# A decoder trunk in split float32: a narrower second product behind the sub-layer borders, a shift split once a sub-layer, and another order of the output's chunks

## The chip, the cores and the metric

The kernel runs on one core of a Trainium2 chip. The time is the device time of one launch in microseconds (us), the median of several runs.

## The reference

Two layers over one sequence of 256 tokens of width 1024. Each layer has three sub-layers: a half-step SwiGLU FFN, a token mixer (layer 0: stick-breaking attention, layer 1: an RG-LRU recurrence) and a second FFN. Each sub-layer is normed and modulated by a conditioning vector `c`:

```python
def sublayer_input(x, g, mod_j):
    shift, scale, gate = mod_j[:, 0], mod_j[:, 1], mod_j[:, 2]
    h = rmsnorm(x, g) * (1 + scale[:, None, :]) + shift[:, None, :]
    return h, (1 + gate)[:, None, :]
...
    for layer in range(DEPTH):
        mod = (c_act @ mod_w[layer] + mod_b[layer]).reshape(B, N_SUB, 3, D_MODEL)
        h, g = sublayer_input(x, norm_g[layer, 0], mod[:, 0])
        x = x + MACARON_W * g * swiglu(h, ffn_w_gu[layer, 0], ffn_w_down[layer, 0])
        h, g = sublayer_input(x, norm_g[layer, 1], mod[:, 1])
        ...
        x = x + g * y
        h, g = sublayer_input(x, norm_g[layer, 2], mod[:, 2])
        x = x + MACARON_W * g * swiglu(h, ffn_w_gu[layer, 1], ffn_w_down[layer, 1])
    return rmsnorm(x, final_norm_g)
```

Everything is float32. About 250 MB of weights are read once.

## The kernel before

**Split products.** Activations lie with the features on the 128 partitions and the 256 tokens along the free axis. A float32 product is made of three products of a 32-bit format that TensorE streams faster ("fp32r"): each operand is split into a high part and a low part, and `group` (L610) issues high weights x high activations, high weights x low activations, low weights x high activations, all into one PSUM bank. Weights come by DMA into `raw`, ScalarE writes the high part `wh` (L581) and VectorE the low part `wl` (L584). Activations of a sub-layer's input are `hx` tiles (with copies of the first of them in `hk`), and what goes into a down projection lies in an arena, `arenar`: the FFN's products `y`, the attention's output, the recurrence's output.

**Borders.** Behind a sub-layer the norm's factor is not known until all of `x` is. `up_first` therefore multiplies the first two weight tiles of the next sub-layer with `x * scale` without the norm, and `evict` multiplies the result with the factor `rst` afterwards (`tr`, L857). The shift, which the norm's factor doesn't touch, rides along in two more columns: `scaled` writes 256 columns of `x * scale` and 2 columns of the shift, so these products have 258 columns (`TX`). ScalarE writes the two high columns, VectorE the two low ones (L720), once for each of the eight chunks of a sub-layer. `evict` reads one of the two result columns as the bias `bc` (L856). There are five such borders, (0,1), (0,2), (1,0), (1,1) and (1,2) as (layer, sub-layer). Each has 2 weight tiles x 8 chunks x 2 halves = 32 groups, 96 matmuls of 258 columns. Meanwhile `rstd` sums the squares, and `norm_chunk` makes the normed input for the weight tiles that follow: `hpre` (L730), its high part on ScalarE, its low part on VectorE (L737).

**The end.** `final` multiplies the eight chunks of `x` by the last norm's factor in five VectorE instructions (`put`, L1386) and stores each by DMA, in turn from SP's and ScalarE's queue.

**Order.** All operations are recorded, and `schedule` sets their order: a list scheduler with a cost for each operation (`c_act`, `c_dve`, `c_mm`) and due times. On ScalarE and VectorE it may hold an engine idle for a more urgent operation that is about to be ready (`wait_for`). TensorE's own order is as recorded.

**Where the tiles lie.** Tiles of the pool `const` are placed one behind the other in each partition, in the order of the listing, and the arena of each phase behind the last of them. Three tiles that nothing uses stand between them:

```python
HXPAD, HKPAD, ARPAD = 112, 16, 56
...
    const.tile([P, HXPAD], F32, tag="pad0", name="pad0")
    hxr, _ = ring("hx", 20, TX, F32R, pitch=320)
    const.tile([P, HKPAD], F32, tag="pad2", name="pad2")
    hkr, _ = ring("hk", 2, T, F32R)
...
    gbias = Buf(ap=fixed("gbias", KD))
    fixed("pad1", ARPAD)
```

In the built program a partition's bytes are: `wh` and `wl` from 43136 (a pitch of 4224, and a view that starts 0 or 128 bytes into the tile, so every one of their views starts at a multiple of 128), `hx` at 102720, `hk` at 128384, `ntri` at 164544, `none` at 165056, `gbias` at 167744, `arenar` at 168000.

Of the kernel before, what the change touches and what calls it, by code (L numbers as in the profile page):

```python
# [130 lines left out]
class Program:  # L131
# [58 lines left out]
    def schedule(self):  # L190
# [61 lines left out]
        def wait_for(e, t, o):  # L252

            q = queue[e]
            while head[e] < len(q) and q[head[e]].start is not None:
                head[e] += 1
            n, i = 0, head[e]
            slack = o.prio + late - t
            while n < LOOK and i < len(q):
                u = q[i]  # L260
                i += 1
                if u.start is not None:
                    continue
                n += 1
                if u is o or u.prio >= o.prio:
                    break
                g = guess(u, 3)
                if g is None or g >= t + o.cost or g <= t:
                    continue
                if u.prio + late - g < o.cost and u.prio + late - g < slack - MARGIN:  # L270
                    return g
            return None
# [123 lines left out]
def c_dve(n):  # L396
    return 68.0 + 1.042 * n
# [11 lines left out]
def trunk(ctx, tc, first_in, cb, par, modw, gu, wdn, qk, wv, wo, win, wri, wout, out):  # L409
# [12 lines left out]
    def f32(ap):  # L422
        return ap.bitcast(F32)
# [74 lines left out]
    def fixed(name, cols, dt=F32):  # L498
        return const.tile([P, cols], dt, tag=name, name=name)
# [51 lines left out]
    def A(o, i, f, n, r, w, table=None, psum=False, ptr=0, after=(), **kw):  # L551
        def fn():
            act.activation(o(), i(), f, **{k: (v() if callable(v) else v) for k, v in kw.items()})  # L553
        return pr.op("ACT", c_act(n, psum, ptr), fn, r, w, after, table)

    def V(fn, n, r, w, cost=None, ptr=0):
        return pr.op("DVE", cost or c_dve(n) + 62.0 * ptr, fn, r, w)

    def load(src, n, name, chain=None, sizes=None, plain=0, homes=(), behind=(), kind=Buf):

# [30 lines left out]
    class Acc:  # L591
# [3 lines left out]
            self.b = Buf(banks, name=name)  # L595
            self.started = False

        def group(self, part, o, w, wc, xs, xc, stop, parts=(None,), passes=(0, 1, 2)):

            b = self.b  # L600
            start = not self.started
            self.started = True
            wh, wl = w
            xh, xl = xs

            def fn():
                seq = ((wh, xh), (wh, xl), (wl, xh))
                for n, i in enumerate(passes):
                    u, v = seq[i]
                    pe.matmul(o(b()), wc(u()), xc(v()), start=start and n == 0, stop=stop and n == len(passes) - 1,  # L610
                              skip_group_check=True)

            n = xs_n[0]
            ws = [wh] * (passes != (2,)) + [wl] * (2 in passes)
            rd = ws + [(t, q) for t in [xh] * (passes != (1,)) + [xl] * (1 in passes) for q in parts]
# [15 lines left out]
    def group(acc, part, o, w, wc, xs, xc, n, stop, parts=(None,), passes=(0, 1, 2)):  # L631
        xs_n[0] = n
        return acc.group(part, o, w, wc, xs, xc, stop, parts, passes)


    def mod_tile(l, s, w, t, after=(), lat=None, rate=RATE, home=None, behind=()):
# [11 lines left out]
    def mod_final(l, s, w, t0=0, n=KD):  # L648
        m, f = mraw[l, s, w], mfin[l, s, w]
        b = OFF_MB + (l * 9 + s * 3 + w) * KD + t0  # L650
        rr = [(m, t) for t in range(t0, t0 + n)]
        ww = [(f, t) for t in range(t0, t0 + n)]
        pp = [(pars, 0)] if l == s == 0 else [pars]
        mi = lambda: m()[:, t0 : t0 + n]
        fo = lambda: f()[:, t0 : t0 + n]
        if w == 0:
            V(lambda: dve.tensor_tensor(fo(), mi(), col(b, n), ALU.add), n, rr + pp, ww)
# [10 lines left out]
    ssq, hcur, gcur, hkick = {}, {}, {}, {}  # L668

    def add_square(gen, d):  # L670
        if d == 0:
# [39 lines left out]

    def scaled(gen, d):

        gs, sh = mfin[gen + (1,)], mfin[gen + (0,)]
# [5 lines left out]
        V(lambda: dve.tensor_tensor(lo()[:, T:], shc(), f32(hi()[:, T:]), ALU.subtract), 2, [(sh, d), (hi, 1)], [(lo, 1)])  # L720
        A(lambda: hi()[:, :T], x[d], AF.Copy, T, [x[d], (gs, d)], [(hi, 0)], ptr=1, scale=lambda: gs()[:, c])
        V(lambda: dve.scalar_tensor_tensor(lo()[:, :T], x[d](), gs()[:, c], f32(hi()[:, :T]), ALU.mult, ALU.subtract), T,
          [x[d], (gs, d), (hi, 0)], [(lo, 0)], ptr=1)

    def norm_chunk(gen, d, q, whole=False):
        gs, sh = mfin[gen + (1,)], mfin[gen + (0,)]
        hp, hi, lo = Buf(hpr), Buf(hxr), Buf(hxr)
        hcur.setdefault(gen, []).append((hi, lo))
        c = slice(d, d + 1)
        V(lambda: dve.scalar_tensor_tensor(hp(), x[d](), gs()[:, c], q(), ALU.mult, ALU.mult), T,  # L730
          [x[d], (gs, d), q] + [(sh, d)] * whole, [hp], ptr=1)
        h = None
        if whole:
            h = Buf(hpr)
            V(lambda: dve.tensor_scalar(h(), hp(), sh()[:, c], None, ALU.add), T, [hp, (sh, d)], [h], ptr=1)
        A(lambda: hi()[:, :T], hp, AF.Identity, T, [hp, (sh, d)], [hi], ptr=1, bias=lambda: sh()[:, c])
        V(lambda: dve.scalar_tensor_tensor(lo()[:, :T], hp(), sh()[:, c], f32(hi()[:, :T]), ALU.add, ALU.subtract), T,  # L737
          [hp, (sh, d), hi], [lo], ptr=1)
        return h

    def norm(gen, q):
# [97 lines left out]
    def up_first(gen, ws, scale=(1.0, 1.0)):  # L839


        gx = gcur.pop(gen)
        accs = {}
        for i, w in enumerate(ws):
            accs[i] = [Acc(f"first_{gen}_{i}_{g}") for g in range(2)]
            for k in range(KD):
                if (i, k) == ((0, 6) if gen == (0, 1) else (1, 0)):
                    q = rstd(gen)
                for g in range(2):
                    c0 = (k % 4) * 256 + g * P  # L850
                    group(accs[i][g], 0, lambda b: b[:, :TX], w[k // 4], lambda u, c0=c0: u[:, c0 : c0 + P], gx[k],
                          lambda v: v, TX, k == KD - 1, parts=(0, 1))

        def evict(i, g):
            b, t, c = accs[i][g].b, Buf(tr), Buf(bcr)
            V(lambda: dve.tensor_scalar(c()[:, :1], b()[:, T : T + 1], scale[g], None, ALU.mult), 1, [b], [c])  # L856
            V(lambda: dve.scalar_tensor_tensor(t(), b()[:, :T], scale[g], q(), ALU.mult, ALU.mult), T, [b, q], [t])  # L857
# [522 lines left out]
    def final():  # L1380
        q = rstd("end")

        def put(d0, n, queue):
            o = xall[:, d0 * T : (d0 + n) * T].rearrange("p (d t) -> p d t", d=n)
            xs = x[d0 : d0 + n]
            V(lambda: dve.tensor_tensor(o, o, q().unsqueeze(1).to_broadcast([P, n, T]), ALU.mult), n * T, xs + [q], xs)  # L1386
# [169 lines left out]
```

## Time and profile before

| | |
|---|---|
| median of 3 runs | 947.73 us (947.19 to 947.96) |
| profiled execution | 947.46 us, its span 945.7 us |
| PE busy | 934.8 us (99%) |
| VectorE (DVE) busy | 781.6 us (83%) |
| ScalarE (ACT) busy | 559.3 us (59%) |
| HBM read | 248.92 MB, 264 GB/s over the span |

The span is the profiled execution from its first instruction to its last. Its own time is 1.8 us more than its span. Busy times of PE are sums of instruction durations with overlaps counted once; matmuls overlap each other, so a matmul's duration is longer than the time from its start to the next one's.

### The profile page before, as it was taken

The numbers are of one execution on the slowest core, as the hardware profiler recorded it, in microseconds if no ns is written. First come the engines' busy times: TensorE is split into PE (matmuls) and PEld (weight loads), VectorE is DVE, ScalarE is ACT, GpSimd is POOL, SyncE is SP. The second block draws the span as 40 slices with busy tenths as digits, with TensorE's granted clock in tenths as the row PEclk, the third lists the DMA queues.
The fourth block names the chain that finished last, engine by engine and source line by source line (L and its number), as shares of the span: only waits on it lengthen the run. The fifth ranks groups of instructions, "written<-read, shape, count | busy, mean of one in ns | idle before, by whom it ended". The sixth has DMA issues, their size and how long they took to land.

```text
span 945.7 us, 19610 instructions
## 1 busy us (share of the span) xinstructions
PE 934.8 (99%) x8078; PEld 924.2 (98%) x8078; DVE 781.6 (83%) x1279; ACT 559.3 (59%) x914; POOL 2.1 (0%) x14
## 2 busy tenths in 40 slices
PE   8999999999999999999999999999999999999996
PEld 6999999999999999999999999999999999999996
DVE  7999888899987989888799998866999997555443
ACT  5785553488785754454367554544789675554343
POOL 0000000000000000000000000000000000000000
PEclk9999999999999999999999999999999999999999
DMA  9989989948833699889967999885253646555421
GB/s 362 404 332 368 340 333 361 364 170 320 294 133 130 269 337 359 319 313 359 348 250 275 346 348 353 327 321 223 90 198 116 223 189 244 192 186 211 170 104 45
DMA packets 48332, 251.25 MB, mean 266 GB/s; under 512 B 5361, under 2 KB 5745, under 8 KB 28530
## 3 DMA queue, kind: packets, MB, share of 16 engines
q1 hardware_dynamic: 47952, 249.59, 70.2%
q8 instruction: 63, 1.03, 0.4%
q10 hardware_dynamic: 290, 0.40, 0.1%
q14 instruction: 27, 0.22, 0.1%
HBM read 248.92 MB, written 1.05 MB: 264 GB/s over the span
## 4 chain that ended last, share of the span: by engine, by line
PE 97%; DVE 2%; DMA 1%; ACT 0%; issue 0%; SPq 0%; DVEq 0%
PE bank L610 90%; PE bank L1041 2%; PE bank L1274 1%; PE bank L916 1%; DMA arenar<-in_first_in 1%; PE bank L1107 1%; PE bank L1168 1%; DVE wl L584 1%; PE bank L1144 1%; DVE arenar L644 0%; DVE x L1386 0%; PE bank L1147 0%; DVE arenaf L1358 0%; PE bank L703 0%; DVE arenaf L1345 0%
## 5 line engine op out<-in xcount | busy, mean ns | idle before, releaser
L610 PE MATMUL bank<-hx,wh 128*128 128x256 f32 (+1 forms) x3264 | 560.4, 277 | 0.0
L581 ACT ACTIVATE wh<-raw 128x1024 fp32r<-128x1024 f32 (+1 forms) x330 | 335.3, 1037 | 281.9 <-PE bank L610 199.0
L610 PEld LDWEIGHTS bank<-hx,wh 128*128 128x128 f32 x3264 | 492.7, 188 | 0.0
L584 DVE TENSOR_TENSOR wl<-raw,wh 128x1024 fp32r<-128x1024 f32 (+1 forms) x330 | 386.6, 1196 | 118.5 <-ACT wh L581 114.8
L610 PE MATMUL bank<-hx,wl 128*128 128x256 f32 (+1 forms) x1640 | 452.7, 277 | 0.0
L610 PEld LDWEIGHTS bank<-hx,wl 128*128 128x128 f32 x1640 | 308.4, 188 | 0.0
L610 PE MATMUL bank<-arenar,wh 128*128 128x256 f32 x1696 | 289.4, 276 | 0.0
L610 PEld LDWEIGHTS bank<-arenar,wh 128*128 128x128 f32 x1696 | 255.4, 188 | 0.2 <-issue 0.2
L610 PE MATMUL bank<-arenar,wl 128*128 128x256 f32 x848 | 234.3, 276 | 0.1
L644 DVE SCALAR_TENSOR_TENSOR rawm<-rawm,cact 128x1024 f32<-128x1024 f32 x128 | 154.7, 1220 | 8.2 <-DMA rawm<-in_modw 8.2
L610 PEld LDWEIGHTS bank<-arenar,wl 128*128 128x128 f32 x848 | 159.2, 188 | 0.3 <-DVE wl L584 0.3
L553 ACT ACTIVATE arenar<-a 128x256 fp32r<-128x256 f32 x88 | 35.3, 405 | 12.6 <-DVE a L869 10.8
L874 DVE TENSOR_TENSOR arenar<-a,arenar 128x256 fp32r<-128x256 f32 x88 | 36.4, 419 | 0.5 <-ACT arenar L553 0.5
L553 ACT ACTIVATE sg<-bank 128x256 f32<-128x256 f32 x82 | 30.0, 369 | 8.3 <-PE bank L610 8.1
L869 DVE TENSOR_TENSOR a<-bank,sg 128x256 f32<-128x256 f32 x82 | 34.1, 418 | 0.7 <-ACT sg L553 0.4
L553 ACT ACTIVATE arenaf<-bank 128x256 f32<-128x256 f32 (+1 forms) x53 | 23.2, 488 | 11.2 <-PE bank L610 5.1
L784 DVE SCALAR_TENSOR_TENSOR x<-bank,mf,x 128x256 f32<-128x256 f32 (+1 forms) x49 | 21.7, 473 | 9.2 <-PE bank L610 9.1
L553 ACT ACTIVATE hx<-x,mf 128x256 fp32r<-128x256 f32 x40 | 19.2, 500 | 16.3 <-DVE x L784 16.3
L553 ACT ACTIVATE hx<-hpre,mf 128x256 fp32r<-128x256 f32 x41 | 20.0, 504 | 11.4 <-DVE hpre L730 10.8
L1041 PE MATMUL bank<-wh,hx 128*128 128x256 f32 x128 | 23.0, 279 | 0.0
L644 DVE SCALAR_TENSOR_TENSOR arenar<-arenar,cact 128x1024 f32<-128x1024 f32 x16 | 19.5, 1221 | 1.9 <-DMA arenar<-in_first_in 1.9
L1496 ACT ACT_TABLE_LOAD x15 | 19.2, 1283 | 1.6 <-PEq L1544 1.3
(124 smaller groups left out, 504.2 us busy)
## 6 DMA issues: line engine op xcount, KB each, us to landing
raw<-in_gu SPq DMA_DIRECT2D x79, 1024.0 KB, 5.5
rawm<-in_modw SPq DMA_DIRECT2D x128, 512.0 KB, 6.9
raw<-in_wdn SPq DMA_DIRECT2D x44, 1024.0 KB, 4.9
raw<-in_win SPq DMA_DIRECT2D x10, 1024.0 KB, 4.9
arenar<-in_first_in SPq DMA_DIRECT2D x16, 512.0 KB, 7.8
raw<-in_qk SPq DMA_DIRECT2D x8, 1024.0 KB, 4.9
raw<-in_wout SPq DMA_DIRECT2D x5, 1024.0 KB, 4.8
raw<-in_first_in SPq DMA_DIRECT2D x8, 512.0 KB, 8.9
```

The source lines that it names most:

```text
L553: act.activation(o(), i(), f, **{k: (v() if callable(v) else v) for k, v in kw.items()})
L581: act.activation(h()[:, :m], raw()[:, a : a + m], AF.Copy)
L584: dve.tensor_tensor(lo()[:, :m], raw()[:, a : a + m], f32(h()[:, :m]), ALU.subtract)
L610: pe.matmul(o(b()), wc(u()), xc(v()), start=start and n == 0, stop=stop and n == len(passes) - 1, skip_group_check=True)
L644: dve.scalar_tensor_tensor(raw(), raw(), 1.0, cact(), ALU.mult, ALU.mult, accum_out=m()[:, t : t + 1])
L784: dve.scalar_tensor_tensor(x[d]()[:, w], acc.b()[:, j * T + w.start : j * T + w.stop], gate()[:, d : d + 1], x[d]()[:, w], ALU.mult, ALU.add)
L869: V(lambda: dve.tensor_tensor(a(), b()[:, T:], sg(), ALU.mult), T, [(b, (1, 0)), sg], [a])
L874: V(lambda: dve.tensor_tensor(y[1](), a(), f32(y[0]()), ALU.subtract), n, [a, y[0]], [y[1]])
L916: pr.op("PE", c_mm(T, 4), lambda: pe.matmul(b()[:, g * T : (g + 1) * T], raw()[:, c0 : c0 + P], h0(), start=start, stop=False, skip_group_ ...
L1041: pe.matmul(o, u()[:, tb * P : (tb + 1) * P], v()[:, c0 : c0 + 256], start=start and n == 0, stop=k == KD - 1 and n == 2, skip_group_check ...
L1107: pe.matmul(zb[e][i]()[:, j * m : (j + 1) * m], y()[rows, kc], y()[rows, qc], start=j == 0, stop=j == 1, skip_group_check=True)
L1496: act.preload_act_table_set(TABLES[t])
```

## The change

It has five parts.

1. The second product of a border's group (high weights x low activations) takes 256 columns instead of 258 (`m=T`).
2. The two extra columns are no longer the high shift twice in the high tile and the low shift twice in the low tile. They are the high and the low shift side by side in the high tile. They are split once a sub-layer in `mod_final`, into new tiles `sh` of 16 columns, five of them, and ScalarE copies two columns of that for each chunk. VectorE's 40 instructions of two columns are gone. `evict` adds the two result columns.
3. `evict` may not run before the last low part of the norm's chunks (`after=[lows[gen]]`).
4. `wait_for` doesn't hold an engine when the wait is longer than the delay that it would save.
5. The output's chunks are multiplied and stored as 1, 2, 2, 2, 1 in this order, not as 1, 1, 2, 2, 2 in an order of the scheduler's choice.

The `sh` tiles stand between `gbias` and the unused tile `pad1`, whose size is as before. In the built program `hx`, `hk`, `wh`, `wl`, `ntri` and `none` lie where they lay, and `arenar` is at 168320.

```diff
-                if g is None or g >= t + o.cost or g <= t:
+                if g is None or g >= t + o.cost or g <= t or t + o.cost - g < g - t:
                     continue
...
     gbias = Buf(ap=fixed("gbias", KD))
+    shr = {(l, q): Buf(ap=fixed(f"sh{l}{q}", 2 * KD, F32R)) for l in range(2) for q in range(3) if l or q}
     fixed("pad1", ARPAD)
...
-                    pe.matmul(o(b()), wc(u()), xc(v()), start=start and n == 0, stop=stop and n == len(passes) - 1,
-                              skip_group_check=True)
+                    c = slice(0, m if i == 1 else None)
+                    pe.matmul(o(b())[:, c], wc(u()), xc(v())[:, c], start=start and n == 0,
+                              stop=stop and n == len(passes) - 1, skip_group_check=True)
...
+            if (l, s) in shr:
+                y = shr[l, s]
+                two = lambda i: y().rearrange("p (d i) -> p d i", i=2)[:, :, i]
+                A(lambda: two(0), fo, AF.Copy, KD, ww, [(y, 0)])
+                V(lambda: dve.tensor_tensor(two(1), fo(), f32(two(0)), ALU.subtract), KD, ww + [(y, 0)], [(y, 1)])
...
-        shc = lambda: sh()[:, c].to_broadcast([P, 2])
-        A(lambda: hi()[:, T:], shc, AF.Copy, 2, [(sh, d)], [(hi, 1)])
-        V(lambda: dve.tensor_tensor(lo()[:, T:], shc(), f32(hi()[:, T:]), ALU.subtract), 2, [(sh, d), (hi, 1)], [(lo, 1)])
+        A(lambda: hi()[:, T:], lambda: f32(y()[:, 2 * d : 2 * d + 2]), AF.Copy, 2, [(y, 0), (y, 1)], [(hi, 1)])
...
-                          lambda v: v, TX, k == KD - 1, parts=(0, 1))
+                          lambda v: v, TX, k == KD - 1, parts=(0, 1), m=T)
...
-            V(lambda: dve.tensor_scalar(c()[:, :1], b()[:, T : T + 1], scale[g], None, ALU.mult), 1, [b], [c])
-            V(lambda: dve.scalar_tensor_tensor(t(), b()[:, :T], scale[g], q(), ALU.mult, ALU.mult), T, [b, q], [t])
+            V(lambda: dve.tensor_scalar(c()[:, :1], b()[:, T : T + 1], b()[:, T + 1 : TX], scale[g], ALU.add, ALU.mult), 1, [b], [c],
+              ptr=1, after=[lows[gen]])
+            V(lambda: dve.scalar_tensor_tensor(t(), b()[:, :T], scale[g], q(), ALU.mult, ALU.mult), T, [b, q], [t],
+              after=[lows[gen]])
...
-        for d0, n, queue in ((0, 1, "SP"), (1, 1, "ACT"), (2, 2, "SP"), (4, 2, "ACT"), (6, 2, "SP")):
+        puts = []
+        for d0, n, queue in ((0, 1, "SP"), (1, 2, "ACT"), (3, 2, "SP"), (5, 2, "ACT"), (7, 1, "SP")):
             put(d0, n, queue)
```

TensorE at the first border, (0,1), before: the last products of the first FFN's down projection and the first two groups of 258 columns (a row with x2 is two instructions).

```order
L610 MATMUL bank_69<-arenar_728,wh_79 128x256 x2
L610 MATMUL bank_69<-arenar_728,wl_86 128x256
L610 MATMUL bank_70<-hx,wh_80 128x258 x2
L610 MATMUL bank_70<-hx,wl_87 128x258
L610 MATMUL bank_64<-hx,wh_80 128x258 x2
L610 MATMUL bank_64<-hx,wl_87 128x258
```

The same place now:

```order
L612 MATMUL bank_69<-arenar_733,wh_79 128x256 x2
L612 MATMUL bank_69<-arenar_733,wl_86 128x256
L612 MATMUL bank_70<-hx,wh_80 128x258
L612 MATMUL bank_70<-hx,wh_80 128x256
L612 MATMUL bank_70<-hx,wl_87 128x258
L612 MATMUL bank_64<-hx,wh_80 128x258
L612 MATMUL bank_64<-hx,wh_80 128x256
L612 MATMUL bank_64<-hx,wl_87 128x258
```

TensorE has the same instructions in the same places; 160 of them have two columns less.

VectorE at the border (0,2), before: the norm's `hpre` and low parts, with the evictions `tr` and `bc` among them.

```order
L730 TENSOR_SCALAR hpre_105<-x,mf_164,rst_102 128x256
L857 TENSOR_SCALAR tr_110<-bank_65,rst_102 128x256
L753 COPY hk_96<-hx 128x256
L856 TENSOR_SCALAR bc_106<-bank_65 128x1
L737 TENSOR_SCALAR hx<-hpre_103,mf_162,hx 128x256
L730 TENSOR_SCALAR hpre_103<-x,mf_164,rst_102 128x256
L857 TENSOR_SCALAR tr_111<-bank_66,rst_102 128x256
L856 TENSOR_SCALAR bc_107<-bank_66 128x1
L737 TENSOR_SCALAR hx<-hpre_104,mf_162,hx 128x256
```

The end of the same stretch now (`hpre` is L735, the low parts L742, `bc` L862, `tr` L864, `wl` L585):

```order
L742 TENSOR_SCALAR hx<-hpre_104,mf_162,hx 128x256
L742 TENSOR_SCALAR hx<-hpre_105,mf_162,hx 128x256
L585 TENSOR_TENSOR wl_85<-raw_73,wh_78 128x1024
L742 TENSOR_SCALAR hx<-hpre_103,mf_162,hx 128x256
L585 TENSOR_TENSOR wl_86<-raw_73,wh_79 128x1024
L585 TENSOR_TENSOR wl_87<-raw_71,wh_80 128x1024
L864 TENSOR_SCALAR tr_110<-bank_65,rst_102 128x256
L862 TENSOR_SCALAR bc_106<-bank_65 128x1
```

The evictions moved behind the last low part, and two weight splits moved ahead of them.

VectorE at the end of the program, before, where it multiplies the output's chunks:

```order
L784 TENSOR_SCALAR x<-bank_66,mf_184,x 128x128 x2
L1386 TENSOR_TENSOR x<-x,rst_102 128x512 x3
L1386 TENSOR_TENSOR x<-x,rst_102 128x256 x2
L1551 UNCONDITIONAL_BRANCH
```

And now:

```order
L790 TENSOR_SCALAR x<-bank_66,mf_184,x 128x128 x2
L1394 TENSOR_TENSOR x<-x,rst_102 128x256
L1394 TENSOR_TENSOR x<-x,rst_102 128x512 x3
L1394 TENSOR_TENSOR x<-x,rst_102 128x256
L1561 UNCONDITIONAL_BRANCH
```

One of the two single chunks moved to the front.

More of the change, by code (lines that the diff above doesn't have):

```diff
@@ L554, in A, with V @@
         return pr.op("ACT", c_act(n, psum, ptr), fn, r, w, after, table)
-    def V(fn, n, r, w, cost=None, ptr=0):
-        return pr.op("DVE", cost or c_dve(n) + 62.0 * ptr, fn, r, w)
+    def V(fn, n, r, w, cost=None, ptr=0, after=()):
+        return pr.op("DVE", cost or c_dve(n) + 62.0 * ptr, fn, r, w, after)
     def load(src, n, name, chain=None, sizes=None, plain=0, homes=(), behind=(), kind=Buf):
@@ L596, in __init__, with group @@
             self.started = False
-        def group(self, part, o, w, wc, xs, xc, stop, parts=(None,), passes=(0, 1, 2)):
+        def group(self, part, o, w, wc, xs, xc, stop, parts=(None,), passes=(0, 1, 2), m=None):
             b = self.b
@@ L609, in fn @@
                     u, v = seq[i]
-                    pe.matmul(o(b()), wc(u()), xc(v()), start=start and n == 0, stop=stop and n == len(passes) - 1,
-                              skip_group_check=True)
+                    c = slice(0, m if i == 1 else None)
+                    pe.matmul(o(b())[:, c], wc(u()), xc(v())[:, c], start=start and n == 0,
+                              stop=stop and n == len(passes) - 1, skip_group_check=True)
             n = xs_n[0]
             ws = [wh] * (passes != (2,)) + [wl] * (2 in passes)
-            rd = ws + [(t, q) for t in [xh] * (passes != (1,)) + [xl] * (1 in passes) for q in parts]
+            rd = ws + [(xh, q) for q in parts if passes != (1,)] + [(xl, q) for q in parts[:1] if 1 in passes]
             if not start:
@@ L629, in group32, with group @@
               [w, x32] + ([] if start else [(b, "start")]), [(b, part)] + ([(b, "start")] if start else []))
-    def group(acc, part, o, w, wc, xs, xc, n, stop, parts=(None,), passes=(0, 1, 2)):
+    def group(acc, part, o, w, wc, xs, xc, n, stop, parts=(None,), passes=(0, 1, 2), m=None):
         xs_n[0] = n
-        return acc.group(part, o, w, wc, xs, xc, stop, parts, passes)
+        return acc.group(part, o, w, wc, xs, xc, stop, parts, passes, m)
     def mod_tile(l, s, w, t, after=(), lat=None, rate=RATE, home=None, behind=()):
@@ L665, in mod_final @@
             V(lambda: dve.tensor_scalar(fo(), mi(), 1.0, wt, ALU.add, ALU.mult), n, rr, ww)
-    ssq, hcur, gcur, hkick = {}, {}, {}, {}
+    ssq, hcur, gcur, hkick, lows = {}, {}, {}, {}, {}
     def add_square(gen, d):
@@ L712, in scaled @@
     def scaled(gen, d):
-        gs, sh = mfin[gen + (1,)], mfin[gen + (0,)]
+        gs, y = mfin[gen + (1,)], shr[gen]
         hi, lo = Buf(hxr), Buf(hxr)
@@ L738, in norm_chunk @@
           [hp, (sh, d), hi], [lo], ptr=1)
+        lows[gen] = pr.ops[-1]
         return h
@@ L1385, in put @@
             xs = x[d0 : d0 + n]
-            V(lambda: dve.tensor_tensor(o, o, q().unsqueeze(1).to_broadcast([P, n, T]), ALU.mult), n * T, xs + [q], xs)
+            puts.append(V(lambda: dve.tensor_tensor(o, o, q().unsqueeze(1).to_broadcast([P, n, T]), ALU.mult), n * T, xs + [q], xs,
+                          after=puts[-1:]))
             if queue == "SP":
```

## The prediction

> **What bounds the kernel now.** I read the page first, then who TensorE waited for, then the chain that ended last, then TensorE's groups by shape, and last a stretch of its timeline. The page says who is busy:
>
> ```profile
> span 945.7 us, 19610 instructions
> PE 934.8 (99%) x8078; PEld 924.2 (98%) x8078; DVE 781.6 (83%) x1279; ACT 559.3 (59%) x914; POOL 2.1 (0%) x14
> ...
> PE 97%; DVE 2%; DMA 1%; ACT 0%; issue 0%; SPq 0%; DVEq 0%
> ```
>
> The last line is the chain that ended last: 97% of it is TensorE. Does TensorE ever wait? The view of its waits (line, whom it waited for, us in total, times, longest) has three rows:
>
> ```profile
> PE bank L916 <- DVE hpre L735: 1.7, 1, 1.7
> PE bank L1407 <- POOL eps L509: 1.2, 1, 1.2
> PE bank L1421 <- DMA rawm<-in_cb: 0.7, 1, 0.7
> ```
>
> All three lie in the start of the program (L1407 and L1421 warm up and condition, L916 is the first product). Behind that TensorE waits for nobody, so the time is the number of matmuls times their pace, plus the start and the tail. Two pieces of the chain, in order of time (start, us, what), give the pace:
>
> ```profile
> 197.93 7.25 PE bank L610 x60
> ...
> 762.45 174.49 PE bank L610 x1536
> ```
>
> The second is the last FFN: 174.49 / 1536 = 113.6 ns from one matmul to the next. The first is half of a border, all of 258 columns: 7.25 / 60 = 120.8 ns. The two columns cost 7.2 ns, far more than 2/256 of 113.6. So the pace moves in a step, and a thing that costs a matmul one such step matters here. TensorE's groups by shape (count, busy us, mean ns of one) show where else it occurs:
>
> ```profile
> L610 PE MATMUL bank<-hx,wl 128*128 128x256 f32 x1488 | 409.6, 276 | 0.0
> L610 PE MATMUL bank<-arenar,wh 128*128 128x256 f32 x1696 | 289.4, 276 | 0.0
> L610 PE MATMUL bank<-arenar,wl 128*128 128x256 f32 x848 | 234.3, 276 | 0.1
> L610 PE MATMUL bank<-hx,wl 128*128 128x258 f32 x152 | 43.1, 284 | 0.0
> L1041 PE MATMUL bank<-wl,hx 128*128 128x256 f32 x64 | 17.7, 277 | 0.0
> L610 PE MATMUL bank<-hk,wl 128*128 128x256 f32 x32 | 9.0, 282 | 0.0
> L610 PE MATMUL bank<-hx,arenar 128*128 128x258 f32 x40 | 5.8, 284 | 0.0
> L1147 PE MATMUL bank<-arenar,none 128*128 128x256 f32 x16 | 3.2, 279 | 0.0
> L1144 PE MATMUL bank<-arenar,ntri 128*128 128x256 f32 x16 | 3.0, 280 | 0.0
> L695 PE MATMUL bank<-hk,none 128*128 128x256 f32 x10 | 2.0, 281 | 0.0
> ```
>
> Compare the rows of 256 columns. `hx` and `arenar` with `wl` take 276 ns, `hk` with the same `wl` takes 282, though `hk` is a plain copy of one `hx` chunk, of the same type and size. What differs is where it lies. By the addresses of the built program, in bytes modulo 128: `wh` and `wl` start at 0, `hx` and `arenar` at 64 (102720, 168000), `hk` at 0 (128384), `ntri` and `none` at 64. Where the moving tile and the weights start at different places modulo 128, a matmul takes 276 or 277: `hx`, `arenar`, and L1041, where the weights are what moves (at 0) and `hx` is held (at 64). Where they start at the same place it takes 279 to 282: `hk` with `wl`, `arenar` with `none` and with `ntri`. One row is against it, `hk` with `none`, 281 with different places; it is ten matmuls that stand in pairs between products of 258. The timeline shows the same as a pace:
>
> ```profile
> 210.71 0.28 PE L610 MATMUL bank<-hk,wl 128*128 128x256 f32 x1
> ...
> 211.43 0.28 PE L610 MATMUL bank<-hx,wl 128*128 128x256 f32 x1
> ...
> 211.77 0.28 PE L610 MATMUL bank<-hx,wl 128*128 128x256 f32 x1
> ...
> 212.45 0.28 PE L610 MATMUL bank<-hx,wl 128*128 128x256 f32 x1
> ```
>
> From 210.71 to 211.43 six matmuls start, mostly of `hk`: 120 ns each. From 211.77 to 212.45 six of `hx`: 113 ns each.
>
> **The arena moves (the term that decides).** Five new tiles of 16 columns x 4 bytes = 320 bytes go in ahead of the arena; the unused tile behind them keeps its size. 320 is two and a half times 128, so every `arenar` tile goes from 64 to 0 modulo 128 (168000 to 168320), which is where `wh` and `wl` start. The arena's tiles then stand to the weights as `hk` does now. This meets 1696 + 848 = 2544 matmuls, all down and output projections, and no other work covers it, since TensorE is the chain. The price of one: 6 ns by the mean durations (282 less 276), 6.7 by the timeline (120 less 113.3). I take 6.5: 2544 x 6.5 = **+16.5 us**. The bounds are the weakest and the strongest neighbour: `none` and `ntri`, 279.5 less 276 = 3.5 ns, +8.9 us; the step of the 258 columns, 284 less 276 = 8 ns, +20.4 us. `hk` is the nearest row: same weights, same type, same 256 columns, same places.
>
> Two small things hang on the same move. At the border (1,0) part of the weights is held in the arena, 64 bytes into its cells: these go from 0 to 64, which is where `hx` starts, for 40 matmuls (the row `hx,arenar`). They pay the step of the 258 columns already; another 6.5 each would be +0.3 us, and nothing is the other bound. The 32 products of `arenar` with `none` and `ntri` of 256 columns part from their weights' place: 32 x 3.5 ns = -0.1 us.
>
> **The narrower product.** 5 borders x 32 groups = 160 matmuls go from 258 to 256 columns. At the full step this is 160 x 7.2 ns = **-1.15 us**. The other bound is 0, if a product of 256 between two of 258 keeps their pace. I take the full step, since the step belongs to a matmul's own columns in all rows above but those of `hk`.
>
> **The shift.** What it removes and adds, and the evictions:
>
> ```profile
> L857 DVE SCALAR_TENSOR_TENSOR tr<-bank,rst 128x256 f32<-128x256 f32 x20 | 8.1, 420 | 0.0
> L720 DVE TENSOR_TENSOR hx<-mf,hx 128x2 fp32r<-128x2 f32 x40 | 4.6, 154 | 1.3 <-ACT hx L553 1.2
> L856 DVE TENSOR_SCALAR bc<-bank 128x1 f32<-128x1 f32 x20 | 2.4, 151 | 0.0
> L657 DVE TENSOR_TENSOR mf<-mr,x 128x8 f32<-128x8 f32 x5 | 0.8, 165 | 0.1
> L553 ACT ACTIVATE hx<-mf 128x2 fp32r<-128x2 f32 x40 | 5.9, 197 | 2.8 <-DVE mf L657 2.8
> ```
>
> VectorE loses 40 x 154 ns = 6.2 us and gains 5 of 8 columns, 5 x 165 = 0.8 us; ScalarE keeps its 40 copies and gains 5 of about 197 ns, 1.0 us. All of it lies beside TensorE's products: three waits of TensorE and none behind the start. On the time I put 0. If that cover were gone, VectorE's 5.4 us would be the gain's bound.
>
> **Evictions behind the low parts, and the scheduler.** At a border four `tr` and four `bc` now stand behind the last low part. Behind them in VectorE's queue are weight splits; who waits for `tr` and `bc` is ScalarE (the sigmoid side of the first two FFN tiles, or the query, or the convolution), and behind that its `wh` splits; the banks that `evict` empties come free later by as much. Before, no TensorE wait came from any of this, and the next weight tiles are split ahead of the evictions now. Price 0; if the cover failed, a border would lose at most its evictions, 4 x (420 + 151) ns = 2.3 us. The rule in `wait_for` only lets an engine go on sooner: also 0.
>
> **The tail.** TensorE has ended; the factor is there at 939.4, and five multiplications and stores follow. Groups of L1386, and the stores (KB each, median us from issue to landing):
>
> ```profile
> L1386 DVE TENSOR_TENSOR x<-x,rst 128x512 f32<-128x512 f32 x3 | 1.9, 687 | 1.9 <-ACT rst L553 1.9
> ...
> L1386 DVE TENSOR_TENSOR x<-x,rst 128x256 f32<-128x256 f32 x2 | 0.8, 419 | 0.0
> ```
>
> ```profile
> out<-x SPq DMA_DIRECT2D x2, 256.0 KB, 2.5
> out<-x ACTq DMA_DIRECT2D x1, 256.0 KB, 2.3
> out<-x SPq DMA_DIRECT2D x1, 128.0 KB, 2.8
> out<-x ACTq DMA_DIRECT2D x1, 128.0 KB, 2.8
> ```
>
> With a single chunk first, the first store goes out 687 - 419 = 0.27 us sooner; the last multiplication ends when it did, since the five are the same. The two last stores, of 128 KB, take longer to land (2.8) than those of 256 KB (2.3 to 2.5), so they stand behind the others, and an earlier start reaches them. I take **-0.25 us**; bounds 0, and -0.5 (2.8 to 2.3).
>
> **The sum**, against the profiled execution's 947.46 us: +16.5 + 0.3 - 0.1 - 1.15 - 0.25 = +15.3, to 962.8. That execution lay 0.27 us below the median of the runs shown, so the forecast as a median is **963.0 us**. The bounds: 8.9 - 0.1 - 1.15 - 0.5 = +7.1, 955 us; 20.4 + 0.3 = +20.7, 968 us.
>
> **The rivals.**
> *The place of a tile costs nothing.* Then `hk` is slow for another reason: it stands at the start of a bank's sum, and its two buffers alternate. For it: only 32 + 64 matmuls, six at a time, and the row of `hk` with `none`. Against it: every sum starts in a new bank, with `hx` or `arenar` as well, and their means are 276; and `none` and `ntri` with `arenar` stay without an explanation. What is left is -1.15 - 0.25 = -1.4, **946.3 us**, not slower by a measurable amount: about 0.2%, 1.9 us, is what a measurement of this kernel can tell from no change. It decides as soon as the price of one matmul is under 1.3 ns (1.4 + 1.9 over 2544). The Trainium skill's page "SBUF — State Buffer", section "Who interferes with whom", states this rule: TensorE has two independent read ports, one for what moves and one for the weights, and never waits on anyone. This trace doesn't agree: 282 against 276 ns between two tiles that differ in their place alone.
> *The evictions become a wait.* Addresses cost nothing, and at every border ScalarE stands before `tr` with the weight splits behind it: five borders x 2.3 us less 1.4 = +10.1, 958 us. Against it: no wait of TensorE's at any border before, and the splits were moved ahead.
> *It doesn't do what it says.* The product of 256 columns between two of 258 keeps 120.8 ns: 1.15 us more than forecast, 964 us; this lies in the range.
>
> **How the numbers follow.** The forecast with its bounds 0.86; addresses cost nothing 0.10 (0.08 within 0.2%, 0.02 faster beyond it, for which the tail and the borders would have to give 0.5 us more than forecast); evictions 0.03; something of TensorE's pace that gains more than all this, faster, 0.01. The range of 955 to 968 holds the first case and the third, and leaves out 0.11. Slower by over 0.2% is 0.86 + 0.03 = 0.89, within it 0.08, faster 0.03.
>
> **What would show it.** Right: `arenar` with `wl` and `wh` (x848, x1696) at about 282 ns instead of 276, `hx` with `wl` still 276, and the last FFN's piece of the chain at about 116 ns a matmul, as 528 of its 1536 are of the arena (113.6 + 6.5 x 528 / 1536); 160 matmuls of 256 columns out of the 480 at borders; still no wait of TensorE's. Wrong: `arenar` at 276 with the time at 946; or a row in TensorE's waits that names `wh` or `wl` behind a border.

## The result, and the profile after

| | before | changed |
|---|---|---|
| median of 5 runs | 947.96 us (947.19 to 949.27) | 975.60 us (974.75 to 976.73) |
| span of the profiled execution | 945.7 us | 972.7 us |

The ratio is 1.0289, with a 95% interval of 1.0274 to 1.0304: slower by 27.6 us. The forecast was 963.0 us and its range ended at 968.

The page of the changed kernel, the same lines as before (span; engines; shares of the chain that ended last), and then TensorE's waits (line, whom it waited for, us in total, times, longest):

```profile
span 972.7 us, 19586 instructions
PE 963.0 (99%) x8078; PEld 952.6 (98%) x8078; DVE 783.0 (81%) x1244; ACT 558.4 (57%) x919; POOL 2.1 (0%) x14
...
PE 98%; DMA 1%; DVE 1%; ACT 0%; SPq 0%; DVEq 0%; issue 0%
```

```profile
PE bank L924 <- DVE hpre L740: 1.3, 1, 1.3
PE bank L1417 <- POOL eps L509: 1.2, 1, 1.2
PE bank L710 <- ACT arenaf L554: 0.4, 1, 0.4
```

Nothing in these lines tells why. TensorE has as many matmuls (8078), is 99% busy in both kernels, and waits 2.9 us in all. VectorE has 35 instructions less and ScalarE 5 more, as said. So the same matmuls take longer, and the groups by shape say which (count, busy us, mean ns of one):

```profile
L612 PE MATMUL bank<-hx,wl 128*128 128x256 f32 x1488 | 414.5, 279 | 0.0
L612 PE MATMUL bank<-arenar,wh 128*128 128x256 f32 x1696 | 305.8, 283 | 0.0
L612 PE MATMUL bank<-arenar,wl 128*128 128x256 f32 x848 | 240.0, 283 | 0.0
L612 PE MATMUL bank<-hx,wl 128*128 128x258 f32 x152 | 42.8, 281 | 0.0
```

`arenar` went from 276 to 283 ns, which was forecast (282). But `hx` with `wl` went from 276 to 279, and `hx` lies where it lay. A mean over 1488 products can be all of them a little slower or some of them much; the chain's pieces and the windows tell. The chain's long pieces (start, us, what):

```profile
313.05 187.85 PE bank L612 x1584
501.14 187.84 PE bank L612 x1584
782.16 182.13 PE bank L612 x1536
```

The last is the last FFN, 182.13 / 1536 = 118.6 ns from one start to the next, where 116 was forecast and 113.6 was before. Now the busy time of TensorE in windows that begin and end with a stretch of like products (stretch: us, PE busy (count), granted clock, DMA share, GB/s). Before, in this order: first FFN's `arenar`, attention's `arenar`, second FFN's `hx`, the border behind it, and the recurrence's `arenar`:

```profile
133.34:193.18 59.84, 59.84 (x530) 1.00 0.90 346
291.56:303.25 11.69, 11.69 (x105) 1.00 0.26 92
315.79:423.93 108.14, 108.14 (x957) 1.00 0.85 321
483.77:495.59 11.82, 11.82 (x100) 1.00 0.41 152
728.90:756.25 27.35, 27.24 (x240) 1.00 0.54 193
```

The same five stretches now:

```profile
132.71:196.05 63.34, 63.34 (x531) 1.00 0.87 333
294.59:306.93 12.34, 12.34 (x104) 1.00 0.25 86
319.31:431.67 112.36, 112.36 (x957) 1.00 0.82 311
495.02:506.68 11.66, 11.66 (x100) 1.00 0.54 206
747.52:776.04 28.52, 28.52 (x241) 1.00 0.49 185
```

A window also counts the two or three products that overlap its edges; 528, 102, 954, 98 and 237 begin in these. So the pace of `arenar` in an FFN went from 59.84 / 528 = 113.3 ns to 63.34 / 528 = 120.0, and that of `hx` in the second FFN from 108.14 / 954 = 113.4 to 112.36 / 954 = **117.8**. The clock is 1.00 throughout. The account:

| stretch | worked out | us |
|---|---|---|
| `arenar`, four FFNs | 4 x (63.34 - 59.84) | +14.0 |
| `arenar`, attention (two stretches) and recurrence | 0.65 + 0.16 + 1.17 | +2.0 |
| `hx`, second, third and fourth FFN | 3 x (112.36 - 108.14) | +12.7 |
| borders | 5 x (11.66 - 11.82) | -0.8 |
| tail, from the first output multiplication | (972.7 - 966.81) - (945.7 - 939.46) | -0.4 |

The sum is +27.5; the spans differ by 27.0. The rest is in the program's start: the first FFN's `arenar` began 0.6 us sooner (132.71 against 133.34). The attention's first stretch changed by only 0.16 us because it was not at the fast pace before either. These are its last 72 products in the chain, before and after, 8.48 / 72 = 117.8 and 8.63 / 72 = 119.9 ns apart:

```profile
281.70 8.48 PE bank L610 x72
```

```profile
284.58 8.63 PE bank L612 x72
```

The tail's starts are those of the timeline, before and after:

```profile
939.46 2.57 DVE L1386 TENSOR_TENSOR x<-x,rst 128x512 f32<-128x512 f32 x5 [1.87 <-ACT rst L553]
```

```profile
966.81 2.56 DVE L1394 TENSOR_TENSOR x<-x,rst 128x256 f32<-128x256 f32 x5 [1.88 <-ACT rst L554]
```

So the forecast's +16.5 for the arena came (+16.0), and 12.7 us came with it that no step of the prediction holds: the `hx` products of three FFNs. In the first FFN `hx` kept 113.4 ns. The same ring of tiles, the same weights' places, two paces in one execution. Not every border slowed what follows it. These pieces of the chain, before and after, are the second half of the border (1,1) and the 96 products behind it; there the change gained 0.1 us:

```profile
670.48 16.77 PE bank L610 x144
```

```profile
689.21 16.67 PE bank L612 x144
```

That is what the experiments are about.

### The profile page after: what moved, and what is told of

The parts are those of the page before. It is cut to its first block, busy times and chain, and to the rows that moved or that the text cites. A ratio compares the mean times of both kernels' runs of the same rounds, so it can differ in the third digit from the quotient of the medians.

```text
span 972.7 us, 19586 instructions
## 1 busy us (share of the span) xinstructions
PE 963.0 (99%) x8078; PEld 952.6 (98%) x8078; DVE 783.0 (81%) x1244; ACT 558.4 (57%) x919; POOL 2.1 (0%) x14
## 4 chain that ended last, share of the span: by engine, by line
PE 98%; DMA 1%; DVE 1%; ACT 0%; SPq 0%; DVEq 0%; issue 0%
PE bank L612 92%; PE bank L1049 2%; PE bank L1282 1%; PE bank L924 1%; PE bank L1115 1%; PE bank L1176 1%; PE bank L1152 1%; DMA arenar<-in_first_in 1%; DVE arenar L646 0%; DVE x L1394 0%; PE bank L1155 0%; PE bank L710 0%; PE bank L702 0%; SPq L547 0%; DVEq L1561 0%; ACT rms L554 0%
## 5 line engine op out<-in xcount | busy, mean ns | idle before, releaser
L612 PE MATMUL bank<-hx,wh 128*128 128x256 f32 (+1 forms) x3264 | 572.7, 280 | 0.0
L585 DVE TENSOR_TENSOR wl<-raw,wh 128x1024 fp32r<-128x1024 f32 (+1 forms) x330 | 388.0, 1195 | 145.0 <-ACT wh L582 139.7
L612 PEld LDWEIGHTS bank<-hx,wl 128*128 128x128 f32 x1640 | 312.2, 190 | 0.0
L612 PE MATMUL bank<-arenar,wh 128*128 128x256 f32 x1696 | 305.8, 283 | 0.0
L612 PEld LDWEIGHTS bank<-arenar,wh 128*128 128x128 f32 x1696 | 264.5, 192 | 0.2 <-issue 0.2
L612 PE MATMUL bank<-arenar,wl 128*128 128x256 f32 x848 | 240.0, 283 | 0.0
L612 PEld LDWEIGHTS bank<-arenar,wl 128*128 128x128 f32 x848 | 162.8, 192 | 0.0
L1049 PE MATMUL bank<-wh,hx 128*128 128x256 f32 x128 | 23.2, 279 | 0.0
```

Of the source, the lines that this page charges most:

```text
L585: dve.tensor_tensor(lo()[:, :m], raw()[:, a : a + m], f32(h()[:, :m]), ALU.subtract)
L612: pe.matmul(o(b())[:, c], wc(u()), xc(v())[:, c], start=start and n == 0, stop=stop and n == len(passes) - 1, skip_group_check=True)
L1049: pe.matmul(o, u()[:, tb * P : (tb + 1) * P], v()[:, c0 : c0 + 256], start=start and n == 0, stop=k == KD - 1 and n == 2, skip_group_check ...
```

## The experiments

Paces below are the time from one product's start to the next, over a whole stretch. Places are in bytes modulo 256: before, `hx` and the arena lie at 64; the change moves the arena to 128; the views of `wh` and `wl` that TensorE holds as weights all start at 128, and no run moves them. The theories:

- *Place*: the place of the moving tile sets a product's pace (the prediction's). It explains `arenar` and not `hx`.
- *Width*: `hx` is slow because the narrow product between two of 258 columns leaves TensorE in a slower pace behind the border.
- *Inheritance*: `hx` takes over the slow pace that the arena's products had ahead of the border.
- *Exit*: only the border's last products count for that.
- *Jump*, *`hk`*: the pace of `hx` comes of how the border's tiles lie to what was before, or of the `hk` products that stand behind the border.
- *State*: TensorE can stream the same products at several paces; it holds the one that it is in until something of another kind comes between.

All in one table (us; paces in ns; the last two columns are FFN stretches, `hx` behind the borders):

| kernel | arena | second product | time | ratio, 95% interval | `arenar` | `hx` |
|---|---|---|---|---|---|---|
| changed | 128 | 256 | 975.6 | 1.0289 (1.0274 to 1.0304) | 120.0 | 117.8 |
| e1 | 192 | 256 | 968.39 | 1.0208 (1.0186 to 1.0230) | 117.8 | 117.8 |
| e2 | 128 | 258 | 963.38 | 1.0169 (1.0154 to 1.0184) | 120.0 | 113.4 |
| e3 (before) | 128 | 258 | 963.63 | 1.0168 (1.0153 to 1.0183) | 120.0 | 113.4 |
| e4 | 192 | 258 | 956.73 | 1.0094 (1.0079 to 1.0109) | 117.8 | 113.4 |
| e5 | 64 | 256 | 947.01 | 0.9993 (0.9976 to 1.0009) | 113.3 | 113.4 |
| e6 | 64 | 258 | 947.63 | 0.9997 (0.9982 to 1.0011) | 113.3 | 113.4 |
| e7 | 64 | 256, last chunk 258 | 947.24 | 0.9987 (0.9965 to 1.0008) | 113.3 | 113.4 |
| e8 (before) | 64 | 258, no `hk` | 947.16 | 0.9990 (0.9975 to 1.0005) | 113.3 | 113.4 |
| e9 | 128 | 256, last chunk 258 | 963.15 | 1.0158 (1.0143 to 1.0173) | 120.0 | 113.4 |
| e10 (`hx` at 192 too) | 192 | 256 | 976.57 | 1.0305 (1.0288 to 1.0322) | 117.8 | 117.8 |
| e11 | 0 | 256 | 968.62 | 1.0214 (1.0199 to 1.0229) | 118.7, 120.0 | 113.4, 117.8 |
| e12 (kicks) | 192 | 256 | 948.42 | 1.0005 (0.9995 to 1.0014) | 113.5 | 113.4 |

In the views below two fixed windows are shown for each kernel: 140 to 190 us lies in the first FFN's `arenar`, 330 to 410 in the second FFN's `hx`. More products in the same time is a faster pace. Before, and after:

```profile
140.00:190.00 50.00, 50.00 (x443) 1.00 0.94 360
330.00:410.00 80.00, 80.00 (x709) 1.00 0.90 337
```

```profile
140.00:190.00 50.00, 50.00 (x419) 1.00 0.88 335
330.00:410.00 80.00, 80.00 (x682) 1.00 0.81 311
```

**e1, the arena 64 bytes further.** It was meant to undo the move, by taking the arena back to 64 modulo 128.

```diff
-HXPAD, HKPAD, ARPAD = 112, 16, 56
+HXPAD, HKPAD, ARPAD = 112, 16, 72
```

> The changed kernel with the unused tile behind the five new ones 16 columns larger, so that the arena starts at 64 modulo 128 bytes again. Place theory (an arena tile at the weights' place costs its matmul one step): arenar's matmuls go from 283 back to 276 ns by their mean, 2544 x 6.5 ns = 16.5 us less. For the rest of the loss, the hx matmuls of the last three FFNs, which start 117.8 ns apart instead of 113.4 (3 x 954 x 4.4 ns = 12.6 us): the width theory (the border's mix of 258, 256 and 258 columns leaves TensorE in a slower pace that lasts until the arena's products) says that they stay at 117.8, time 975.6 - 16.5 = 959 us. The inheritance theory (they take over the slow pace of the arena's products before the border) says that they go back to 113.4, time 946.5 us.

```profile
132.96:195.15 62.19, 62.19 (x531) 1.00 0.92 341
293.31:304.98 11.67, 11.67 (x104) 1.00 0.28 91
330.00:410.00 80.00, 80.00 (x681) 1.00 0.83 310
```

968.39 us, a miss for both theories. The first two rows are the first FFN's and the attention's `arenar`: 62.19 / 528 = 117.8 ns, and 11.67 us against 11.69 before, so the old pace. One arena, one place, two paces in one execution, and the slow one is neither 113.4 nor 120.0. And 64 modulo 128 was too coarse a name for the place: 192 is not 64. The second row ends at the border (0,2) and the third lies behind it: `hx` is slow here behind an arena that ran fast, so *inheritance* does not account for it. One of the four runs took 965.0 us, the others 968.2 to 968.7; the trace is of one of the latter.

**e2, the second product wide again**, by two columns of zeros in the low tile; the rest of the change stays.

```diff
+        if True:
+            two = lambda: f32(y()[:, 2 * d : 2 * d + 2])
+            V(lambda: dve.tensor_tensor(lo()[:, T:], two(), two(), ALU.subtract), 2, [(y, 0), (y, 1)], [(lo, 1)])
...
-                          lambda v: v, TX, k == KD - 1, parts=(0, 1), m=T)
+                          lambda v: v, TX, k == KD - 1, parts=(0, 1), m=None)
```

> The changed kernel with the second product of a border's groups at 258 columns again; the low tile's two columns are written as zeros for that by VectorE, 40 instructions of two columns. The arena stays where the change put it. Width theory: hx behind the borders back to 113.4 ns from start to start, time 975.6 - 12.6 + 0.8 = 964 us. Inheritance theory: hx stays at 117.8, 976 us. Both: arenar stays at 120 ns.

```profile
140.00:190.00 50.00, 50.00 (x419) 1.00 0.91 337
330.00:410.00 80.00, 80.00 (x709) 1.00 0.87 330
```

963.38 us: `arenar` stays at 120 ns, `hx` is back (709 as before). *Inheritance* falls. The narrow product, which saves 0.8 us at the borders, costs 12.7 behind them here.

**e3, the arena alone moved, in the kernel before**: the same line as in e1, which there puts the arena at 128.

> The kernel before with the unused tile 16 columns larger and nothing else, so that the arena starts at 0 modulo 128 bytes. Place theory with width theory: arenar at 120 ns from start to start, hx at 113.4, time 947.9 + 16.5 = 964.4 us. With the inheritance theory: hx of three FFNs at 117.8 as well, 977 us. If the place costs nothing: 948 us.

963.63 us, with `arenar` at 120.0 and `hx` at 113.4 ns. The move by itself costs 963.63 - 947.6 (the kernel before, measured beside it) = 16.0 us. No product and no instruction differs from the kernel before, only the size of a tile that nothing uses: the place alone does this.

**e4, both of e1 and e2.**

> The changed kernel with both undone: the arena at 64 modulo 128 bytes and the second product at 258 columns (low tile's two columns written as zeros). What is left of the change is the shift split once, the evictions behind the low parts, the scheduler's rule and the output's order. Width and inheritance theory alike: arenar and hx both at 113.4, time about 947.9 - 0.25 (the tail) = 947.6 us. A time clearly above 948.5 would mean a third cause among the parts left.

956.73 us, not the time before: `hx` is fast, `arenar` in the FFNs runs at 117.8. So 192 is a place with a price of its own.

**e5, the arena back at 64 modulo 256, second product narrow.**

```diff
-HXPAD, HKPAD, ARPAD = 112, 16, 56
+HXPAD, HKPAD, ARPAD = 112, 16, 40
```

> The changed kernel with the unused tile 16 columns smaller, so that the arena starts at 168256, which is 64 modulo 256 bytes as before (168384 was 192). Theory of 256 bytes: what counts is the place modulo 256, so the FFN's arenar products go from 117.8 to 113.4 ns a start. Width theory for hx behind the FFN's borders: still 117.8. Time 975.6 - 16.5 = 959 us. If a third part of the change slows the arena's products, arenar stays at 117.8: 968 us as with the arena at 168384. If both slow paces have one cause, the place modulo 256, hx is at 113.4 too: 947 us.

```profile
140.00:190.00 50.00, 50.00 (x443) 1.00 0.94 360
330.00:410.00 80.00, 80.00 (x708) 1.00 0.87 326
```

947.01 us, every FFN stretch at 113.4 ns, `hx` behind the narrow borders too. *Width* by itself falls: with the arena at 64 the narrow borders leave `hx` fast. What hurts the FFNs is both together, the moved arena and the narrow border. How they act together isn't shown. That the arena's pace ahead of a border doesn't decide is seen in e1, and here as well: behind the border (0,1) 42 products of L1049 (the prediction's L1041: the weights move, `hx` is held) took 4.95 / 42 = 117.9 ns each in e5, where the arena ahead ran at 113.3, and 4.77 / 42 = 113.6 in the changed kernel, where it ran at 120.0. e5, then the changed kernel:

```profile
205.00 4.95 PE bank L1049 x42
```

```profile
207.88 4.77 PE bank L1049 x42
```

**e6, e5 with the wide product, and e7, e5 with it in the last chunk only.** e7's edit is that of e2 under `d == KD - 1`, with `m=None if k == KD - 1 else T`.

> The same place of the arena (64 modulo 256), and the second product at 258 columns with zeros in the low tile's two columns. Theory of 256 bytes with width theory: all long stretches at 113.4, time 947.6 - 0.4 (the tail as the changed kernel's trace shows it) = 947.2 us. If a third part slows the arena: 956.7 us as with the arena at 168384.

> The same place of the arena, and the second product at 256 columns except for the last of the eight chunks, where it has 258 (zeros in that chunk's low columns). Exit theory (what sets the pace behind a border is how its last products end, not the narrower products as such): hx behind the borders at 113.4, time 947.2 - 0.7 = 946.5 us. If any narrow product in a border sets the slow pace: hx at 117.8, 959 us.

947.63 and 947.24 us. With the arena at 64 the FFN stretches run at 113.4 ns whatever the border does, so e7 can't tell whether the border's last products count; e9 was made for that. Wide and narrow borders can now be compared at three places of the arena: 947.63 and 947.01 at 64, 956.73 and 968.39 at 192, 963.38 and 975.6 at 128.

**e8, the kernel before without `hk`** at the tile behind an FFN's border.

```diff
-            up(acc, ..., (l, s), f == (f0 + 1 if j == 0 else f0))
+            up(acc, ..., (l, s), j == 0 and f == f0 + 1)
```

> The kernel before, with the first up projection behind the FFN's borders reading the first chunk from hx and not from its copy hk, which lies at the weights' place. The copies are still made. If the six products of hk are what brings TensorE back into the fast pace behind the products of 258 columns: hx of the three FFNs at 117.8, time 947.6 + 12.6 = 960 us. If they only cost their own step: 947.6 - 3 x 6 x 6.5 ns = 947.5 us.

947.16 us, `hx` at 113.4 ns with `hk` and without. Behind the old borders it isn't the `hk` products that bring the pace back.

**e9, the changed kernel with the last chunk wide**: e7's edit with the arena at 128. Of a border's 32 second products, 4 are wide again, and the border ends on 12 products of 258 columns.

> The changed kernel with the arena where the change put it (128 modulo 256) and the second product at 258 columns in the last of the eight chunks of a border only (12 of its 96 matmuls in a row end as before). Exit theory: the end of the border brings hx back to 113.4 ns a start, arenar stays at 120, time 963 us. If it takes a border that is all of 258 columns: hx at 117.8, 975 us.

```profile
140.00:190.00 50.00, 50.00 (x420) 1.00 0.91 337
330.00:410.00 80.00, 80.00 (x708) 1.00 0.86 327
```

963.15 us: `arenar` as in the changed kernel, `hx` fast. *Exit* holds with the arena at 128: the last twelve products of a border decide the pace of the 954 behind it.

**e10, `hx` and the arena both at 192 modulo 256.**

```diff
-HXPAD, HKPAD, ARPAD = 112, 16, 56
+HXPAD, HKPAD, ARPAD = 144, 16, 40
```

> The changed kernel with hx and the arena both at 192 modulo 256 (hx was at 64); the weights stay at 128. Jump theory (the slower pace of 117.8 comes from a change of the moving tiles' place between hx and the arena, not from a place): all long stretches at 113.4, 947 us. Theory of 256 bytes (192 is a bad place): hx and arenar both at 117.8, over 3 x 954 + 954 + 2544 matmuls, 975 us or more.

```profile
70.00:130.00 60.00, 60.00 (x512) 1.00 0.90 337
140.00:190.00 50.00, 50.00 (x427) 1.00 0.91 345
330.00:410.00 80.00, 80.00 (x681) 1.00 0.86 317
```

976.57 us. The first row lies in the first FFN's `hx`, where the kernel before has 532 products and no border has been yet. All of it runs at 117.8, though `hx` and the arena share one place. *Jump* falls, and at 192 the slow pace comes without a border or an arena ahead of it.

**e11, the arena at 0 modulo 256**, the same modulo 128 as the changed kernel's 128 (`ARPAD` 24).

> The changed kernel with the arena at 0 modulo 256, that is at the weights' place modulo 128 but not modulo 256. If the step of the same place counts modulo 128: arenar at 120 ns a start, hx behind the borders at 117.8, 975.6 us as the changed kernel. If it counts modulo 256: arenar at 113.4 or 117.8, 947 to 968 us.

968.62 us. In the FFNs `arenar` runs at 118.7 ns in two and at 120.0 in the other two; `hx` at 113.4 behind the border (0,2) and at 117.8 behind (1,0) and (1,2). Neither expectation came out as written. One kernel shows both outcomes of a narrow border, and `arenar` is at 120.0 in just those FFNs whose `hx` was slow. So here the pace of `arenar` goes with that of the `hx` stretch right ahead of it. The pace of `hx` does not go with that of the arena ahead of its border: ahead of (0,2) and (1,2) it was 118.7 both times.

**e12, e1 with a tiny product of another kind between.** It adds seven products of 64 bf16 columns of zeros, behind the first group of a down projection and of the first full weight tile behind an FFN's border. The kernel calls such a product a kick, and holds six of them at other places before and after the change.

```diff
+                if kick and k == 1 and g == 0 and gen in ((0, 2), (1, 0), (1, 2)):
+                    kick_op(acc, 0, (0, 0))
...
-             lambda k: (ys[k], slice(0, T)), 2, lambda c: hook(NF + 2 * c), kicks=())
+             lambda k: (ys[k], slice(0, T)), 2, lambda c: hook(NF + 2 * c), kicks=(0,))
```

> The changed kernel with the arena at 168384 (192 modulo 256), which took 968.4 us, and a product of 64 columns of zeros (38 ns) put in at seven places: behind the first group of the FFNs' down projections and in the first full weight tile behind the FFNs' borders. State theory (the slow pace is one of two that the same matmuls at the same places can hold, and a disturbance can change it): some of the long stretches go from 117.8 to 113.4; all of them would give 947.3 us. Place theory: no stretch changes, 968.7 us.

The timeline at one of them, behind the border (0,2) (start, us, what), and the two windows:

```profile
316.46 0.28 PE L612 MATMUL bank<-hx,wl 128*128 128x256 f32 x1
316.58 0.20 PE L844 MATMUL bank<-ident,zero 128*128 128x64 bf16 x1
316.62 0.48 PE L612 MATMUL bank<-hx,wh 128*128 128x256 f32 x2
```

```profile
140.00:190.00 50.00, 50.00 (x444) 1.00 0.94 358
330.00:410.00 80.00, 80.00 (x709) 1.00 0.86 325
```

948.42 us against e1's 968.39, each beside the kernel before. The product occupies 0.04 us of TensorE (316.58 to 316.62), and the 951 behind it run at 113.4 ns where they ran at 117.8. Same tiles, same places, same products around: *state* is shown: the same products at the same places have two paces, and what is done ahead of them has a say in which. At 128 such a product didn't help. In the changed kernel one of the six stands behind the first three products of the recurrence's output, and the 237 behind it took 28.52 / 237 = 120.3 ns each:

```profile
747.48 0.20 PE L842 MATMUL bank<-ident,zero 128*128 128x64 bf16 x1
```

No version beat the kernel before measurably. e5 keeps the whole change, with the unused tile 16 columns smaller, and is level with it at a ratio of 0.9993 (0.9976 to 1.0009).

## Why the prediction was wrong

- **TensorE is the chain, and its pace is the time**: held. The view of its waits names none behind the start in either kernel.
- **The arena moves, +16.5 us**: held in sign and size, and in that the place alone does it (e3). 2544 products took 16.0 us more, 6.3 ns each, where 6.5 was taken from `hk`. Its bounds were 8.9 and 20.4. The rival that a tile's place costs nothing falls with e3. The rule of the Trainium skill, page "SBUF — State Buffer", section "Who interferes with whom" (TensorE's two read ports are independent and it never waits), leaves no room for the 16.0 us; that it is these ports that collide, no run shows.
- **"`hx` with `wl` still 276"**: this is the step that failed. The prediction read the pace as a property of a product's own tiles, so tiles that didn't move could cost nothing. The runs show in its place that the same product at the same place has more than one pace, that a pace lasts, and that what ran ahead has a say in which one it is. `hx` behind three narrow borders ran at 117.8 ns: +12.7 us, where the median missed the forecast by 12.6. Undoing any one of three things ends that: the narrow product (e2), its last chunk alone (e9), or the arena's move (e5). Why the moved arena and the narrow border slow `hx` only together stays open; taking over the arena's pace is ruled out (e1, e2). Two rows before the change spoke against the prediction's reading. `hk` with `none`, at 281 ns though the places differ, was set aside as a special case. The chain's piece of 72 `arenar` products at 117.8 ns, with the arena still at 64, was left out. Both were signs that place does not settle a pace by itself. Nor do `hk` and `hx` behind an FFN's border differ in place alone, as the prediction says: in e8, where `hx` stands in the place of `hk` in that run of products, the first three still start 119.7 ns apart.
- **The same place as the weights, modulo 128**: not the rule. 64 and 192 are alike modulo 128, and e5 and e1 differ by 21 us; at 192 the arena isn't at the weights' place by either count, and `arenar` is slow in the FFNs (e4). The price held because `hk`, from which it was taken, lies at 128 modulo 256 as the moved arena does.
- **The narrower product, -1.15 us**: -0.8 at the borders themselves. A product of 256 columns between two of 258 didn't quite get the full step: 11.66 / 98 = 119.0 ns a product, where full steps would leave (11.82 - 32 x 0.0072) / 98 = 118.3. Not that term but what it does to the products behind the border was missing, and no rival had it.
- **The shift, the evictions and the scheduler, 0**: held. No TensorE wait came at any border.
- **The tail, -0.25 us**: -0.4. The two 128 KB stores from SP's queue land in 2.2 us (median), where SP's had taken 2.8:

```profile
out<-x ACTq DMA_DIRECT2D x2, 256.0 KB, 2.5
out<-x SPq DMA_DIRECT2D x2, 128.0 KB, 2.2
out<-x SPq DMA_DIRECT2D x1, 256.0 KB, 2.2
```

- **The range**: its upper end came from pricing the known places at the dearest neighbour. It had no case in which products that the change doesn't touch become slower, so 968 was no bound.

## What to carry to other kernels

Where TensorE never waits, compare the pace by shape and by stretch (windows with their counts) and not the busy share, which was 99% at 947 us and at 976. After adding any tile, look at where the moving tiles now start, modulo 256 bytes, and shift an unused tile until it is as it was: 16 columns of padding were worth 28 us here. Products of an unlike kind between long runs of like ones are not only a cost, since they can end a slow pace; before one is made cheaper, look at the pace of what follows it.

## What the runs showed of the hardware

In these traces, back-to-back fp32r products of 256 columns have at least four paces at a granted clock of 1.00: 113.4, 117.8, 118.7 and 120.0 ns. The weights lay at 128 modulo 256 in all runs. Arena tiles at 64 held 113.4 in all FFNs (e5 to e8), at 192 they held 117.8 (e1, e4), at 0 118.7 or 120.0 (e11), and at 128 120.0 (changed, e2, e3, e9). The place does not exclude another pace: at 64 a run of 72 products of the attention's output went at 117.8 in the kernel before, and at 192 the FFNs' arena went at 113.5 behind a product of another kind (e12). A pace lasts for hundreds of products: 954 at 117.8 behind one border, and one product of 0.04 us ends it.

Four things stay open: what in TensorE holds a pace; whether a place counts by itself or against the weights, which were never moved; why a border that ends on 258 columns returned `hx` to 113.4 ahead of all three FFNs wherever the arena lay, while one of 258, 256, 258 did so ahead of all three with the arena at 64, ahead of one with it at 0, and ahead of none with it at 128 or 192; and whether anything but the place ends the pace of 120.0 at 128, where one product of another kind did not.
